# Hybrid decoder layer with 16 experts: the offset tables of the dynamic expert blocks made in the second block instead of the first

## The chip, the cores and the metric

One core of one Trainium2 chip runs the whole layer as one program. The metric is device time in microseconds, the median of several executions. Engines: PE (TensorE), DVE (VectorE), ACT (ScalarE), POOL (GpSimd, which here also issues nearly all transfers of the expert stage) and SP (SyncE).

## The reference, cut to what matters

The layer adds three mixers and an output projection to x and then a mixture of experts. Only the experts' stage is touched by the change:

```python
def hier_moe(h, wg, bg, we, be, w_gate, w_up, w_down):
    ...  # top-1 group of 4, then top-2 of its 4 experts: gates (T, 16), two nonzero per token
    for e in range(N_EXPERTS):
        hid = jax.nn.silu(t @ w_gate[e]) * (t @ w_up[e])
        y = y + gates[:, e:e + 1] * (hid @ w_down[e])
```

There are 1024 tokens of width 1024, 16 experts of width 256, float32 throughout.

## The kernel before, in words

The last quarter of the kernel is the expert stage. A token goes to two experts, so 2048 (token, expert) pairs are sorted on the chip into blocks of 128 pairs with one expert each. `moe` lists 23 blocks: four static ones (the first block of experts 0 to 3, known when the kernel is built) and 19 dynamic ones in `ORDER`, where P is an expert with two blocks and S an expert with one; which expert each of these is comes out of the routing. So 19 sets of expert weights are used (numbers 0 to 3 static, 4 to 18 dynamic), each of three 1 MB arrays: gate, up and down.

`moe_run` handles a block a in these steps. `gather(a)` (L1252, POOL) fetches the block's 128 tokens by an indirect transfer. `moe_xt` (L1263) transposes them on PE, and ACT and DVE split them in a high and a low half (L127, L128; the kernel multiplies float32 as three products of halves). `moe_gu` (L1277) is 24 matmuls with the gate and up weights, numbered n = 0 to 23; before number n it calls `mid(n)`. `moe_ht` and `moe_down` (L1289, L1305) transpose the result and multiply it with the down weights; ACT and DVE scale it into a page y (L1308, L1309); POOL adds the page into the output by an indirect transfer that accumulates (L1310, called a scatter below). While block a is multiplied, `splits(a+2)` splits the weights of a later expert into halves: ACT makes the high half (L127), DVE the low one by a subtraction (L128), and POOL makes one of the low halves of the down weights. `mw` holds four pairs of split buffers, so a split waits until PE has read the pair it replaces.

Raw weights land in a ring of ten 1 MB buffers (`raw_tile`, L1191). The first ten arrays are loaded by SP long before; all others are issued by POOL (L1212 for expert 3's up and down, L1217 for the dynamic ones), each waiting until the buffer that it overwrites has been split. `issue_after(K.last_gather)` keeps a group of loads behind the newest gather or scatter on POOL.

`route_map` makes the tables of the dynamic blocks in two parts. The first part (L1140 to L1180, before the first block) is a chain of small operations on DVE that ends in `sel`. The second part, after the `yield` (L1181), is `run(late)`: PE multiplies the slot table by `sel` and `selS` (L1120) and by two row vectors (L1185, L1186), DVE turns the results into offsets and gates (L1112 to L1130) and into `erow`, the experts' row numbers (L1188). Dynamic gathers need `og`; dynamic loads need a register loaded from `erow` (L1215); every scatter needs the offsets and gates, the static blocks' too.

The order on PE is the written order (`manual_schedule`, L1429). On ACT, DVE and POOL a planner sets the order at build time; each engine then works through its instructions in that order. In `moe_run` the second part of `route_map` and `loads(4)` stand in `mid` of block 0 at n = `MAP_AT` = 8 (L1362 to L1364); `loads(5)` stands at the end of block 0 and `loads(6)` at the end of block 1 (L1379, L1380).

Of the kernel before, what the change touches and what calls it, by code (L numbers as in the profile page):

```python
# [41 lines left out]
HT_AT = 12  # L42
ORDER = 'PSSPSSPSSPSSSSS'
YP = [0, 0, 0, 1]
MAP_AT = 8
DOWN_AT = 16
END_POOL = 6
END_PAGE = 3
# [214 lines left out]
def run(gen):  # L263
    for _ in gen:
        pass
# [832 lines left out]
def warm(K, n):  # L1098
    d = K.psum.tile([128, 1024], FT, name="warm", tag="sc")
    for m in range(n):  # L1100
        K.nc.tensor.matmul(d[:, :512].rearrange("p (a b) -> p a b", b=128), K.identb,
                           K.maskb.unsqueeze(1).to_broadcast([128, 4, 128]), start=True, stop=True)
# [146 lines left out]
def moe_gather(K, j):  # L1249
    nc = K.nc  # L1250
    xg = K.xpage.tile([128, D], FT, name="xg", tag="pg")
    K.last_gather = nc.gpsimd.indirect_dma_start(out=xg, out_offset=None, in_=K.td,  # L1252
                                 in_offset=bass.IndirectOffsetOnAxis(ap=K.slots[j][0], axis=0)).ins
    return xg


def moe_xt(K, xg, parts=1):
    nc = K.nc
    xT = [K.op.tile([128, KT, 128], FR, name="xT", tag="mx", bufs=4) for _ in range(2)]
    xv = xg.rearrange("p (d k) -> p k d", k=KT)  # L1260
    pt = K.psum.tile([128, KT, 128], FT, name="pt", tag="sc")
    for k in range(KT):
        nc.tensor.transpose(pt[:, k, :], xv[:, k, :], K.ident)  # L1263
    for z in range(parts):
        ks = slice(z * KT // parts, (z + 1) * KT // parts)
        split(K, xT[0][:, ks], xT[1][:, ks], pt[:, ks])
    return xT


def moe_gu(K, W, xT, mid):  # L1270
    nc, mp = K.nc, K.mp
    ps = K.psum.tile([128, 512], FT, name="pgu", tag="acc", bufs=2)
    order = [(k, t) for hf in range(2) for t in range(2) for k in range(hf * 4, hf * 4 + 4)] + [(k, 2) for k in range(KT)]
    for n, (k, t) in enumerate(order):
        mid(n)
        a, b = passes(xT, W[k // 4])[t]
        nc.tensor.matmul(ps, a[:, k, :], b[:, k % 4].rearrange("p a f -> p (a f)"), start=(n == 0), stop=(n == 23))  # L1277
    sg = mp.tile([128, 256], FT, name="sg", bufs=2)
    nc.scalar.activation(sg, ps[:, :256], AF.Silu)
    nc.vector.tensor_tensor(sg, sg, ps[:, 256:], op=OP.mult)  # L1280
    return sg


def moe_ht(K, hid):
    nc, mp = K.nc, K.mp
    hv = hid.rearrange("p (d k) -> p k d", k=2)
    pt = K.psum.tile([128, 4, 128], FT, name="pth", tag="tr")
    for k in range(2):
        nc.tensor.transpose(pt[:, k, :], hv[:, k, :], K.ident)  # L1289
    hT = [mp.tile([128, 2, 128], FR, name="hT", bufs=4) for _ in range(2)]  # L1290
    split(K, hT[0], hT[1], pt[:, :2, :])
    return hT


def moe_down(K, W, hT, j, spare=False):
    nc, mp = K.nc, K.mp
    yp = K.xpage if spare or YP[K.ny % len(YP)] else K.ypage
    K.ny += 1
    y = yp.tile([128, D], FT, name="y", tag="pg")
    wd = [z.rearrange("p a b c -> p (a b c)").rearrange("p (k d) -> p k d", k=2) for z in W[2]]  # L1300
    py = K.psum.tile([128, 1024], FT, name="py", tag="sc")
    for c in range(2):
        for t, (a, b) in enumerate(passes(hT, wd)):
            for k in range(2):
                nc.tensor.matmul(py[:, c * 512:(c + 1) * 512], a[:, k, :], b[:, k, c * 512:(c + 1) * 512],  # L1305
                                 start=(k == 0 and t == 0), stop=(k == 1 and t == 2))
    gt = K.slots[j][2]
    nc.scalar.activation(y[:, :512], py[:, :512], AF.Copy, scale=gt)  # L1308
    nc.vector.tensor_scalar(y[:, 512:], py[:, 512:], gt, None, op0=OP.mult)  # L1309
    K.last_gather = nc.gpsimd.indirect_dma_start(out=K.out, out_offset=bass.IndirectOffsetOnAxis(ap=K.slots[j][1], axis=0),  # L1310
                                 in_=y, in_offset=None, bounds_check=S + 127, compute_op=OP.add).ins


def moe_run(K, tiles, ex, main):
    n = len(tiles)
    first = {}
    for a, (l, j) in enumerate(tiles):
        first.setdefault(l, a)
    begins = {a: l for l, a in first.items()}
    xg, xT, hid = {}, {}, {}  # L1320

    def gather(a):
        if a < n:
            xg[a] = moe_gather(K, tiles[a][1])

    def loads(l):
        if l in first:
            if l >= len(ex):
                ex.append(Expert(K, None, tiles[first[l]][1] - NSTAT))
            with K.tc.issue_after(K.last_gather):  # L1330
                ex[l].loads()

    def splits(a):
        if a in begins:
            ex[begins[a]].splits(main and a >= n - END_POOL)

    def down(a):
        moe_down(K, ex[tiles[a][0]].W, hid[a], tiles[a][1], main and a >= n - END_PAGE)

    for a in range(3):  # L1340
        gather(a)
    if main:
        late = route_map(K)
        next(late)
        warm(K, WARM[2])
        xT[0] = moe_xt(K, xg[0], 2)
    with ExitStack() as st:
        for ins in [K.last_gather] + ([K.last_tab] if main else []):
            st.enter_context(K.tc.issue_after(ins))
        for l in range(3):  # L1350
            loads(l)
        splits(0)
        loads(3)
        splits(1)
        if not main:
            loads(4)
    if not main:
        xT[0] = moe_xt(K, xg[0], 2)
    for a in range(n + 1):
        if a < n:  # L1360
            def mid(m):
                if main and a == 0 and m == MAP_AT:  # L1362
                    run(late)
                    loads(4)  # L1364
                if m == HT_AT and a > 0:
                    hid[a - 1] = moe_ht(K, hid[a - 1])
                if m == XT_AT and a + 1 < n:
                    xT[a + 1] = moe_xt(K, xg[a + 1])
                if m == DOWN_AT and a == n - 1 and a > 0:
                    down(a - 1)  # L1370

            hid[a] = moe_gu(K, ex[tiles[a][0]].W, xT[a], mid)
            gather(a + 3)
            splits(a + 2)
        else:
            hid[n - 1] = moe_ht(K, hid[n - 1])
        if a > 0 and (a != n - 1 or DOWN_AT is None):
            down(a - 1)
        if a + 2 in begins:  # L1379
            loads(begins[a + 2] + 3)  # L1380


def moe(K, ex):
    tiles = [(l, l) for l in range(NSTAT)]
    p, q = 0, 2 * NPAIR
    for l, c in enumerate(ORDER, NSTAT):
        if c == "P":
            tiles += [(l, NSTAT + p), (l, NSTAT + p + 1)]
            p += 2
        else:  # L1390
            tiles.append((l, NSTAT + q))
            q += 1
    moe_run(K, tiles, ex, True)


def moe_rest(K, a=0):
    rv = K.nc.values_load(K.erow[0:1, NDYN + a:NDYN + a + 1], min_val=0, max_val=1)  # L1397
    with K.tc.If(rv > 0):
        moe_run(K, [(x - a, NSTAT + NALW + x) for x in range(a, NDYN - NALW if a else 1)], [], False)
        if not a:  # L1400
            moe_rest(K, 1)
# [204 lines left out]
```

## Time and profile before

| | |
|---|---|
| time, median of 3 runs | 940.19 us (939.62 to 940.92) |
| the profiled execution: its time | 938.4 us |
| the profiled execution: its span, first to last instruction | 936.7 us |
| mean granted TensorE clock | 0.941 |
| PE busy over the span | 827.5 us (88%) |
| DVE, ACT, POOL busy | 648.7, 494.5, 164.9 us |
| HBM read, written | 97.33 MB, 20.97 MB |

The expert stage lies between about 666 us and the end. The page's slices show shares of busy time in fortieths of the span (23.4 us each); in the timelines a row is a run of like instructions: start and length in us, engine, line, operation, tiles, shape and count, then in brackets how long the engine sat idle before and what released it. A q behind a queue or engine's name means its sequencer. One software queue (q0) carries all that POOL issues.

### The profile page before, as it was taken

How to read it: one execution, taken by the hardware profiler on the slowest of the kernel's cores; microseconds unless marked ns; L12 is line 12 of the kernel's file. 1: busy time of each engine (PE TensorE's matmuls, PEld its weight loads, DVE VectorE, ACT ScalarE, POOL GpSimd, SP SyncE). 2: the span in 40 equal slices, each digit the busy share in tenths (PEclk: the TensorE clock that was granted, in tenths of full speed). 3: DMA queues.
4: the chain of work that ended last, by engine and by line, in shares of the span. 5: the costliest groups of instructions: out<-in, count | busy, mean ns of one | idle time of the engine just before them, and what ended most of it. 6: DMA issues, size and time to landing. Idle time of an engine off the chain costs nothing. (4 is left out here: it accounts for less than half of the span.)

```text
span 936.7 us, 14405 instructions
## 1 busy us (share of the span) xinstructions
PE 827.5 (88%) x5300; PEld 721.2 (77%) x5300; DVE 648.7 (69%) x1442; ACT 494.5 (53%) x1095; POOL 164.9 (18%) x165
## 2 busy tenths in 40 slices
PE   5999999789778998899878899999889999999870
PEld 4999989688667987788767687888568888888760
DVE  6841556988997667767857666766768677787860
ACT  6743516114246665667757554232648677676740
POOL 5100000000000000000000000000446667664221
PEclk9999989669879999999988999999989999999995
DMA  8210100102002002001111218435389999998942
GB/s 266 72 45 2 47 1 25 39 1 57 12 0 69 1 1 68 1 1 40 61 30 49 91 68 330 187 129 209 119 319 327 331 362 309 371 311 293 333 70 47
DMA packets 46008, 119.30 MB, mean 127 GB/s; under 512 B 6670, under 2 KB 26220, under 8 KB 38636
## 3 DMA queue, kind: packets, MB, share of 16 engines
q0 software_dynamic: 13392, 73.41, 23.9%
q1 hardware_dynamic: 28588, 39.05, 12.8%
q10 hardware_dynamic: 3952, 5.86, 1.7%
q8 instruction: 44, 0.72, 0.3%
q14 instruction: 32, 0.26, 0.1%
HBM read 97.33 MB, written 20.97 MB: 126 GB/s over the span
## 5 line engine op out<-in xcount | busy, mean ns | idle before, releaser
L1277 PE MATMUL pgu<-mw,xT 128*128 128x512 f32 x552 | 140.9, 404 | 0.7 <-ACT xT L127 0.7
L128 DVE TENSOR_TENSOR mw<-mraw,mw 128x1024 fp32r<-128x1024 f32 x100 | 119.2, 1230 | 11.7 <-ACT mw L127 11.6
L1277 PEld LDWEIGHTS pgu<-mw,xT 128*128 128x128 f32 x552 | 102.8, 190 | 24.5 <-ACT xT L127 0.9
L127 ACT ACTIVATE mw<-mraw 128x1024 fp32r<-128x1024 f32 x114 | 113.7, 1051 | 15.0 <-PE pgu L1277 14.9
L249 PE MATMUL psA<-wh,hnh 128*128 128x384 f32 (+1 forms) x320 | 110.4, 345 | 1.0 <-ACT wh L127 0.9
L249 PE MATMUL psA<-wl,hnh 128*128 128x384 f32 (+1 forms) x320 | 109.9, 343 | 1.0 <-DVE wl L128 1.0
L249 PE MATMUL psA<-wh,hnl 128*128 128x384 f32 (+1 forms) x320 | 110.5, 345 | 0.2 <-DVE hnl L128 0.2
L879 PE MATMUL psO<-woh,mx 128*128 128x512 f32 (+1 forms) x272 | 87.1, 397 | 3.3 <-DVE mx L128 2.3
L584 DVE SCALAR_TENSOR_TENSOR mix<-mix,par 128x994 f32<-128x994 f32 (+29 forms) x60 | 75.9, 1265 | 2.1 <-ACT mix L581 1.3
L940 POOL IOTA iota<- 128x128 f32 x1 | 0.2, 238 | 434.9 <-DVE mix L612 434.9
L1305 PE MATMUL py<-mw,hT 128*128 128x512 f32 x276 | 67.4, 392 | 4.5 <-DVE y L1309 2.9
L1305 PEld LDWEIGHTS py<-mw,hT 128*128 128x128 f32 x276 | 51.7, 188 | 16.8 <-ACT hT L127 3.9
L249 PEld LDWEIGHTS psA<-wh,hnh 128*128 128x128 f32 x320 | 63.3, 198 | 1.6 <-ACT wh L127 1.3
L249 PEld LDWEIGHTS psA<-wl,hnh 128*128 128x128 f32 x320 | 63.3, 198 | 1.2 <-DVE wl L128 1.2
L249 PEld LDWEIGHTS psA<-wh,hnl 128*128 128x128 f32 x320 | 63.2, 197 | 0.6 <-DVE hnl L128 0.4
L716 DVE TENSOR_REDUCE nm<-sc 128x1 f32<-128x128 f32 (+7 forms) x64 | 46.9, 753 | 21.6 <-PE sc L712 17.8
L718 ACT ACTIVATE e<-sc,nm 128x128 f32<-128x128 f32 (+7 forms) x64 | 47.3, 740 | 25.5 <-DVE nm L716 21.7
L879 PEld LDWEIGHTS psO<-woh,mx 128*128 128x128 f32 x272 | 49.9, 192 | 12.7 <-DVE mx L128 2.8
L258 PE MATMUL psA<-hnh,wl 128*128 128x256 f32 x192 | 57.2, 298 | 0.0
L258 PE MATMUL psA<-hnl,wh 128*128 128x256 f32 x192 | 57.1, 297 | 0.0
L258 PE MATMUL psA<-hnh,wh 128*128 128x256 f32 x192 | 56.1, 292 | 0.2 <-DVE mix L554 0.2
L879 PE MATMUL psO<-wol,mx 128*128 128x512 f32 (+1 forms) x136 | 53.5, 394 | 0.0
(391 smaller groups left out, 1857.6 us busy)
## 6 DMA issues: line engine op xcount, KB each, us to landing
mraw<-in_expert_w_up_dram POOLq DMA_DIRECT2D x16, 1024.0 KB
mraw<-in_expert_w_down_dram POOLq DMA_DIRECT2D x16, 1024.0 KB
mraw<-in_expert_w_gate_dram POOLq DMA_DIRECT2D x15, 1024.0 KB
wraw<-in_w_in_dram SPq DMA_DIRECT2D x64, 128.0 KB
mix<-in_x_dram SPq DMA_DIRECT2D x8, 512.0 KB
wraw<-in_w_out_dram SPq DMA_DIRECT2D x16, 256.0 KB
h<-in_x_dram SPq DMA_DIRECT2D x8, 512.0 KB
out_dram<-h SPq DMA_DIRECT2D x8, 512.0 KB
```

The lines of the kernel that those rows point to most:

```text
L127: K.nc.scalar.activation(hi, src, AF.Copy)
L128: (eng or K.nc.vector).tensor_tensor(lo, src, hi.bitcast(FT), op=OP.subtract)
L249: nc.tensor.matmul(ps[:, :n], a[:, k, cs], b[:, k % 2, :n], start=(k == 0 and t == 0), stop=(k == KT - 1 and t == 2))
L258: nc.tensor.matmul(ps, a[:, k % 2, c0:c0 + 128], b[:, k, :], start=(k == 0 and t == 0), stop=(k == KT - 1 and t == 2))
L584: nc.vector.scalar_tensor_tensor(y[:, sh:], z[:, :S - sh], w(t), y[:, sh:], op0=OP.mult, op1=OP.add)
L716: nc.vector.tensor_reduce(nm, scs[m][:, :n], axis=AX.X, op=OP.max, negate=True)
L718: nc.scalar.activation(e[:, :n], scs[m][:, :n], AF.Exp, bias=nm, accum_out=sums[:, u, m:m + 1])
L879: nc.tensor.matmul(ps, a[:, k, :], b[:, k % 4, c0 % 512:c0 % 512 + c1 - c0], start=(k == 0 and t == 0), stop=(k == KT - 1 and t == 2))
L940: g.iota(t, allow_small_or_imprecise_dtypes=True, **kw)
L1277: nc.tensor.matmul(ps, a[:, k, :], b[:, k % 4].rearrange("p a f -> p (a f)"), start=(n == 0), stop=(n == 23))
L1305: nc.tensor.matmul(py[:, c * 512:(c + 1) * 512], a[:, k, :], b[:, k, c * 512:(c + 1) * 512], start=(k == 0 and t == 0), stop=(k == 1 and t ...
```

## The change

The second part of `route_map` moves from block 0 (before matmul 8 of its gate and up product) to block 1 (before matmul 2). `loads(4)` goes with it. `loads(5)` is traced right behind it instead of at the end of block 0. `loads(6)` stays at the end of block 1. The computation is the same.

```diff
-MAP_AT = 8
+MAP_AT = 2
...
     for a in range(n + 1):
         if a < n:
             def mid(m):
-                if main and a == 0 and m == MAP_AT:
+                if main and a == 1 and m == MAP_AT:
                     run(late)
                     loads(4)
+                    loads(5)
                 if m == HT_AT and a > 0:
                     hid[a - 1] = moe_ht(K, hid[a - 1])
...
-        if a + 2 in begins:
+        if a + 2 in begins and not (main and a == 0):
             loads(begins[a + 2] + 3)
```

## Rows read from the trace of the kernel before

**Rows 1.** The page's second part: busy tenths in 40 slices, PE and DMA.

```profile
PE   5999999789778998899878899999889999999870
DMA  8210100102002002001111218435389999998942
```

**Rows 2.** Stretches, PE from 679 us: engines' busy us (instructions), PEclk, DMA share, GB/s.

```profile
679.00:683.50 4.50, 0.18 (x1) 0.02 (x1) 4.09 (x14) 0.00 (x0) 2.19 (x2) 1.00 0.88 299
683.50:690.30 6.80, 6.79 (x27) 6.02 (x28) 1.37 (x10) 0.99 (x1) 3.31 (x4) 0.50 0.81 306
```

**Rows 3.** Timeline of PE, the first two blocks and one later half block.

```profile
677.05 2.14 PE L1277 MATMUL pgu<-mw,xT 128*128 128x512 f32 x8 [0.69 <-ACT xT L127]
683.51 1.02 PE L1120 MATMUL pio<-sel,tab 128*128 128x27 f32 x4 [4.33 <-DVE sel L1180]
...
685.49 2.08 PE L1277 MATMUL pgu<-mw,xT 128*128 128x512 f32 x4
687.36 1.91 PE L1263 MATMUL pt<-ident,xg 128*128 128x128 f32 x8
688.92 6.48 PE L1277 MATMUL pgu<-mw,xT 128*128 128x512 f32 x24
695.94 1.06 PE L1263 MATMUL pt<-ident,xg 128*128 128x128 f32 x8
696.75 3.05 PE L1277 MATMUL pgu<-mw,xT 128*128 128x512 f32 x12
...
702.40 2.98 PE L1277 MATMUL pgu<-mw,xT 128*128 128x512 f32 x12
705.22 0.39 PE L1289 MATMUL pth<-ident,sg 128*128 128x128 f32 x2
```

**Rows 4.** Timeline of POOL, the scatters at the end.

```profile
863.14 2.27 POOL L1310 DMA_INDIRECT out_dram<-y,os  x1 [8.97 <-DVE mw L128]
864.86 1.17 POOL L1217 DMA_DIRECT2D mraw<-in_expert_w_gate_dram  x1
...
882.41 1.65 POOL L1310 DMA_INDIRECT out_dram<-y,os  x1 [8.62 <-DMA out_dram<-y,os]
...
919.63 1.55 POOL L1310 DMA_INDIRECT out_dram<-y,os  x1 [5.41 <-issue]
```

**Rows 5.** Timeline of PE, its last matmuls.

```profile
908.09 3.02 PE L1305 MATMUL py<-mw,hT 128*128 128x512 f32 x12 [0.47 <-ACT hT L127]
```

**Rows 6.** Stretches, POOL alone: us, POOL busy (instructions), PEclk, DMA share, GB/s.

```profile
692.00:717.00 25.00, 14.90 (x13) 1.00 0.96 335
717.00:738.00 21.00, 12.68 (x10) 1.00 1.02 351
...
758.00:763.00 5.00, 3.84 (x5) 1.00 1.01 428
...
863.00:869.50 6.50, 4.01 (x4) 1.00 0.59 118
```

**Rows 7.** Timeline of DVE, the tables and the next subtractions.

```profile
683.13 0.24 DVE L1180 TENSOR_SCALAR sel<-iota,mz 128x27 f32<-128x27 f32 x1
...
684.77 0.17 DVE L1130 COPY ow<-pio 128x27 f32<-128x27 f32 x1
...
692.85 2.36 DVE L128 TENSOR_TENSOR mw<-mraw,mw 128x1024 fp32r<-128x1024 f32 x2 [1.26 <-ACT mw L127]
```

**Rows 8.** Timeline of POOL, dynamic gathers, loads and the first scatter.

```profile
685.04 1.02 POOL L1252 DMA_INDIRECT xg<-td,og  x1 [3.85 <-DVE ow L1130]
...
694.37 0.56 POOL L1217 DMA_DIRECT2D mraw<-in_expert_w_up_dram  x1 [3.85 <-DVE mw L128]
...
709.20 1.66 POOL L1310 DMA_INDIRECT out_dram<-y,ss  x1 [0.16 <-issue]
```

**Rows 9.** Timeline of POOL, a subtraction and the scatter behind it.

```profile
817.10 2.94 POOL L128 TENSOR_TENSOR mw<-mraw,mw 128x1024 fp32r<-128x1024 f32 x1 [1.12 <-ACT mw L127]
820.21 1.63 POOL L1310 DMA_INDIRECT out_dram<-y,os  x1 [0.17 <-issue]
```

## The prediction

> **What bounds the kernel now.** I read three views in this order: the slices of the page, the timeline of PE around the code that moves, and then, because PE is not the whole story, the timeline of POOL to the end.
>
> The slices show PE at eight or nine tenths through the expert stage and the transfer engines at nine in the same slices [rows 1]. Both could be the limit. The timeline of PE shows what the change aims at: after eight matmuls of block 0, PE stands still for 4.33 us until DVE has made `sel` [rows 3]. The stretches add a second cost of that gap: the granted clock was 1.00 while PE stood, and 0.50 (1.2 instead of 2.4 GHz) from 683.5 to 690.3 [rows 2]. Eight transposes took 1.91 us there and 1.06 later, four matmuls 2.08 us against 2.82 for twelve (702.40 to 705.22) [rows 3].
>
> But PE does not end the kernel. Its last matmuls end at 911.11 [rows 5]; the last scatter is issued 8.5 us later, at 919.63 [rows 4]. The scatters form a chain of their own: one waited 8.62 us on POOL for the transfer of the one before it [rows 4]. How long a scatter takes depends on the loads in front of it in the one queue that POOL fills, and that queue is full: share 1.02 from 717 to 738 [rows 6]. So the end is set by the queue and the chain of scatters. A gain on PE counts only as far as it lets the queue start its work earlier or fills holes in it.
>
> **What the change takes away on PE.** In place of 677.05 to 696.75 (the start of block 1's second half) I lay the same work at full speed [rows 3]: 24 matmuls of block 0 at 2.82 per twelve, 5.64; transposes of block 1, 0.81 (695.94 to 696.75); two matmuls of block 1, 0.47; the tables at their old price, 1.98 (683.51 to 685.49); ten matmuls, 2.35; two transposes, 0.39; eight more, 0.81. That is 12.45, so the second half of block 1 would start at 689.5 instead of 696.75: 7.2 us earlier. If the tables also run at the high clock, their half of the price is gone and it is 8.2. I expect no half clock, since nothing like a 4.33 us stop is left.
>
> Against this stands DVE. `sel` was ready at 683.37 [rows 7]; PE would ask for it at 677.05 + 0.1 + 5.64 + 0.81 + 0.47 = 684.1, so that wait is gone. But block 1's split of xT and the subtractions of expert 1's second half, 1.2 us each [rows 7], now fall into the same microseconds as DVE's part of the tables. In the order that the planner gives DVE, none, one or two of these can stand in front: 0 to 2.4 us, and PE waits for DVE within the tables. I take 1 us, near the lower half, since each is short and the operations of the tables come first in the code. PE gains 5 to 8 us, 6.7 as the middle value.
>
> **What it adds: the tables come later.** The first dynamic gather waited 3.85 us on POOL for `ow` and went at 685.04 [rows 8], 1.5 us after the tables began at 683.51 [rows 3]. Now they begin at 684.1, 0.6 later, or more with a DVE operation in front; at the high clock the two products before `ow` take less. So the gathers and the loads behind them on POOL start 0.2 to 3 us later; I take 0.9, 0.6 and a share of one subtraction. `loads(4)` and `loads(5)` are three transfers each, both groups behind the same gather; the register loads before them move along. What waits in front of them on POOL is only what waited there before. Nothing is short of weights for it: blocks 0 to 3 use loads that are already issued.
>
> **What the queue can use.** From 692 to 717 it moved 335 GB/s for 25 us, 8.4 MB [rows 6]. This is the stretch in which the later loads wait for subtractions that PE paces: the up load of expert 4 stood 3.85 us for one [rows 8]. With PE 6.7 us ahead these waits go, and the queue has always something to do. At the 351 GB/s of the full stretch behind it [rows 6] the 8.4 MB need 23.9 us: 1.1 us saved. But that stretch holds two scatters to six loads, the earlier one only one (the first is issued at 709.20 [rows 8]), and loads alone ran at 428 GB/s [rows 6], at which 8.4 MB need 19.6: 5.4 us saved. One scatter and a few gathers stand between; the estimate from both ends is 3.2 us. The queue's late start (0.9) is to be taken off that: 2.3.
>
> Further on one place is left where PE held the chain: the scatter at 820.21 was issued right behind a subtraction on POOL that had waited 1.12 us for ACT [rows 9]. ACT's splits follow PE's reads, so this wait ends earlier too; 0 to 1.1, I take 1.0. All else from 717 on is queue and chain, and moves along.
>
> The sum: 0.9 - 3.2 - 1.0 = -3.3 us. The profiled execution took 938.4 us and would take 935.1. It lies 1.8 us under the median of the runs; from 940.19 the same sum gives 936.9. PE's 6.7 us are more than twice that; the rest becomes lead of PE over the scatters and comes back as waits for pages at the end.
>
> **Rivals.**
>
> *PE is the bound after all.* If the chain follows PE because the queue has holes enough, the whole 5 to 8 us arrive: 940.2 - 6.7 = 933.5. For it speaks that PE is at nine tenths [rows 1], against it the 8.5 us at the end in which PE does nothing [rows 4, 5].
>
> *The queue gives nothing.* With the lower end (1.1 us), tables 2 us late and nothing at 820 the sum is +0.9; with 1.0 at 820 it is -0.1. That is 939 to 941, no change. For it speaks the share of 0.96 already between 692 and 717 [rows 6].
>
> The Trainium skill has a rule that speaks for this rival: DMA: Bandwidth & Descriptors, "Rules for kernel authors", says that an accumulating transfer next to another access of the same bytes must wait for the semaphore of the earlier one. By that rule the scatters can never overlap, whatever PE does, and the trace agrees (the 8.62 us wait for the scatter before [rows 4]).
>
> *Loads stand behind a waiting scatter (slower).* The change alters the order in which loads, gathers and scatters are traced, and with it the times by which the planner orders POOL. At 863.14 a scatter had kept POOL for 8.97 us and the loads of an expert stood behind it [rows 4]; the queue ran dry, share 0.59 for 6.5 us, 2.7 us lost [rows 6]. Each further place of this kind costs 2.7. One costs most of the gain (939.6); from the second on the kernel is slower: -3.3 + 5.4 = +2.1, 942.3. The same holds for the tables: if the first dynamic gather goes later than 685.04 + 3.2 + 1.0 = 689.2, the late start outweighs what the queue can use. For it speaks that POOL works strictly in its order; against it that only the first loads are moved, and by less than a block.
>
> That the change doesn't do what it says is not likely on PE, whose order is written by hand.
>
> **Chances.** The forecast (934.5 to 938.3) 0.53; the whole of PE's gain (932 to 934.5) 0.09; no change 0.21; slower 0.17. The smallest difference that the measurement of this kernel can tell is about 0.2%, 1.9 us. Faster by more than that is the forecast nearly whole and the first rival, 0.60; within it 0.22; slower 0.18. The range reaches from 932.5, below which half of the first rival lies, to 942.5, above which about half of the slower case lies. The forecast's own range is 934.5 to 938.3: tables 0.2 to 2 us late, 2 to 5 us out of the queue.
>
> **What the profile after would show.** On PE: 24 matmuls of block 0 and the transposes of block 1 without a gap, the tables at about 684 with a wait under 1 us, no stretch of clock 0.50 near 685, the second half of block 1 at 689 to 691. On POOL: the first dynamic gather at 685.3 to 688, the loads of expert 4 with no wait for a subtraction, the first scatter about 6 us earlier. From 692 on a share of 1.0 and more than 335 GB/s. At the end the last scatter near 916.3, and pages waited for longer than before on ACT or PE. I would be wrong if the first gather came after 689, if the low clock stayed, if the queue between 692 and 717 stayed at 335 GB/s, or if the queue had a new hole like the one at 863.

## The result, and the profile after

The changed kernel takes 947.03 us (median of 14 runs, 941.67 to 952.85), the kernel before in the same comparison 939.9 us (14 runs, 934.15 to 944.65). The ratio is 1.0081, with a 95% interval of 1.0054 to 1.0107: slower by 0.8%, where 936.9 us and a small gain had been forecast. The profiled execution took 946.58 us, its span is 945.0 us (before 936.7).

The page's second part for the changed kernel, busy tenths of PE and of the transfer engines; compare [rows 1]:

```profile
PE   5999999789678998999797999999899999999940
DMA  8210101102002002002203129362589898988942
```

PE is still at nine tenths in the expert stage; the transfer engines fall under nine in more slices than before. What the change aims at did happen. The timeline of PE (start, length, engine, line, operation, shape, count, and in brackets the idle time before with what ended it), to be laid beside [rows 3] and [rows 5]:

```profile
675.59 3.07 PE L1277 MATMUL pgu<-mw,xT 128*128 128x512 f32 x12 [0.69 <-ACT xT L127]
...
682.66 0.52 PE L1120 MATMUL pio<-sel,tab 128*128 128x27 f32 x4
...
684.17 0.21 PE L1185 MATMUL per<-sel,e 128*1 128x27 f32 x2 [0.56 <-DVE ow L1130]
...
687.83 3.05 PE L1277 MATMUL pgu<-mw,xT 128*128 128x512 f32 x12
...
906.62 3.01 PE L1305 MATMUL py<-mw,hT 128*128 128x512 f32 x12 [0.47 <-ACT hT L127]
```

And two stretches of PE around the tables (us, PE busy, granted clock, share of the transfer engines, GB/s), against [rows 2]:

```profile
683.00:686.00 3.00, 2.44 (x17) 1.00 0.16 68
686.00:690.00 4.00, 4.00 (x24) 1.00 0.57 166
```

The stop of 4.33 us is gone, the half clock too (1.00 instead of 0.50), and the second half of block 1 starts 12.24 us after block 0's first matmul (687.83 less 675.59) instead of 19.70. PE is 7.5 us ahead. At the end nothing of it is left: PE's last matmuls end at 909.63, 234.0 us after block 0's first one, just as before (911.11 less 677.05 is 234.1), and the last scatter goes only 18.3 us after that, where it went 8.5 us after it [rows 4, 5]. So the time has to be looked for on POOL and in its queue. POOL's timeline in the changed kernel, at the head of the dynamic blocks, in the middle and at the end:

```profile
684.21 2.07 POOL L1252 DMA_INDIRECT xg<-td,og  x1 [5.61 <-DVE tk L1124]
...
689.44 2.42 POOL L128 TENSOR_TENSOR mw<-mraw,mw 128x1024 fp32r<-128x1024 f32 x1
691.80 0.58 POOL L1217 DMA_DIRECT2D mraw<-in_expert_w_gate_dram  x1
...
700.11 2.46 POOL L1310 DMA_INDIRECT out_dram<-y,ss  x1 [0.17 <-issue]
...
716.63 1.80 POOL L1310 DMA_INDIRECT out_dram<-y,ss  x1 [6.02 <-DVE sg L1280]
...
811.38 1.94 POOL L1310 DMA_INDIRECT out_dram<-y,os  x1 [2.57 <-DMA out_dram<-y,os]
813.75 2.95 POOL L128 TENSOR_TENSOR mw<-mraw,mw 128x1024 fp32r<-128x1024 f32 x1 [0.44 <-ACT mw L127]
817.36 0.99 POOL L1252 DMA_INDIRECT xg<-td,og  x1 [0.66 <-PE pt L1263]
825.20 3.27 POOL L128 TENSOR_TENSOR mw<-mraw,mw 128x1024 fp32r<-128x1024 f32 x1 [6.85 <-ACT mw L127]
828.64 1.58 POOL L1310 DMA_INDIRECT out_dram<-y,os  x1 [0.17 <-issue]
829.70 1.16 POOL L1217 DMA_DIRECT2D mraw<-in_expert_w_gate_dram  x1
...
921.17 1.56 POOL L1310 DMA_INDIRECT out_dram<-y,os  x1 [5.27 <-DMA out_dram<-y,os]
927.95 1.56 POOL L1310 DMA_INDIRECT out_dram<-y,os  x1 [5.23 <-issue]
```

The first scatter goes at 700.11, 24.5 us after block 0's first matmul and 7.6 us earlier than before (709.20 less 677.05 is 32.2 [rows 8]). The second goes at 41.0 (716.63), where 41.7 had been the place before, so the lead lasts for one scatter (it takes 15.7 us to land, 7.9 before). From there the scatters fall behind. The worst place is the one at 828.64: it stands behind two subtractions of POOL and a gather, and the second subtraction waited 6.85 us for ACT's half of the split; the loads of the next expert (829.70) stand behind the scatter in turn. From the scatter before it, 17.3 us pass; the same step took 10.9 us before (809.29 to 820.21, [rows 9]).

Not all of that is the subtraction. A transfer has landed with the last update of its semaphore, which the trace has too; for the scatter at 811.38, issued behind three gathers, the view of the output's transfers says:

```profile
DMA to landing us min/median/max: 13.2/13.2/13.2
```

So it landed at 824.6, most of the 6.85 us passed while it was still under way, and the next scatter went 4.1 us after the landing. In the kernel before, these two parts are 9.1 and 1.9 us. POOL alone in a stretch, as in [rows 6]:

```profile
692.00:717.00 25.00, 13.62 (x14) 1.00 0.98 361
...
825.00:830.00 5.00, 4.63 (x3) 1.00 0.01 3
```

The queue is dry there (share 0.01). Two lines of the list of POOL's waits (what waited, for what: us in total, times, longest). The kernel before:

```profile
POOL out_dram L1310 <- DMA out_dram<-y,os: 23.4, 5, 8.6
...
POOL mw L128 <- ACT mw L127: 1.1, 1, 1.1
```

The changed kernel:

```profile
POOL out_dram L1310 <- DMA out_dram<-y,os: 45.2, 9, 9.3
POOL mw L128 <- ACT mw L127: 19.4, 7, 6.9
```

The second line is what is new: subtractions that wait for ACT, 19.4 us instead of 1.1. The first overstates the change, since the list puts some waits of a scatter for the one before it down to DVE or to nothing; all waits of scatters together are 81 us before and 86 after. Nothing in the diff touches the subtractions that wait, which lie 52 to 143 us behind the tables (the first that waits over 1 us goes at 734.43, the last at 825.20). What put them where they wait is the order on POOL.

### The profile page after: what moved, and what is told of

Read it like the earlier page. It is cut to its first block, busy times and chain, and to the rows that moved or that the text cites. A ratio compares the mean times of both kernels' runs of the same rounds, so it can differ in the third digit from the quotient of the medians.

```text
span 945.0 us, 14383 instructions
## 1 busy us (share of the span) xinstructions
PE 826.8 (87%) x5300; PEld 718.0 (76%) x5300; DVE 656.3 (69%) x1442; ACT 495.2 (52%) x1095; POOL 160.0 (17%) x165
## 5 line engine op out<-in xcount | busy, mean ns | idle before, releaser
L128 DVE TENSOR_TENSOR mw<-mraw,mw 128x1024 fp32r<-128x1024 f32 x100 | 128.3, 1323 | 11.6 <-ACT mw L127 10.7
L127 ACT ACTIVATE mw<-mraw 128x1024 fp32r<-128x1024 f32 x114 | 113.5, 1050 | 16.5 <-PE pgu L1277 11.3
L716 DVE TENSOR_REDUCE nm<-sc 128x1 f32<-128x128 f32 (+7 forms) x64 | 46.9, 752 | 19.5 <-PE sc L712 15.7
L879 PEld LDWEIGHTS psO<-woh,mx 128*128 128x128 f32 x272 | 50.4, 194 | 12.8 <-DVE mx L128 2.7
## 6 DMA issues: line engine op xcount, KB each, us to landing
mraw<-in_expert_w_gate_dram POOLq DMA_DIRECT2D x15, 1024.0 KB, 10.4
```

Of the source, the lines that this page charges most:

```text
L127: K.nc.scalar.activation(hi, src, AF.Copy)
L128: (eng or K.nc.vector).tensor_tensor(lo, src, hi.bitcast(FT), op=OP.subtract)
L716: nc.vector.tensor_reduce(nm, scs[m][:, :n], axis=AX.X, op=OP.max, negate=True)
L879: nc.tensor.matmul(ps, a[:, k, :], b[:, k % 4, c0 % 512:c0 % 512 + c1 - c0], start=(k == 0 and t == 0), stop=(k == KT - 1 and t == 2))
```

## What the planner did with the change

Read off the two traces, POOL's order from the second scatter on (S: scatter of a block, G: gather, g, u, d: loads of an expert's gate, up and down, M: POOL's subtraction for an expert; block and expert by number). Before:

```
S1 g7 u7 d7 M4 S2 G8 G9 G10 S3 g8 u8 d8 M5 G11 S4 g9 u9 d9 M6 S5 g10 u10 d10 M7
S6 G12 G13 G14 S7 g11 u11 d11 M8 G15 S8 g12 u12 d12 M9 S9 g13 u13 d13 M10
S10 G16 G17 G18 M11 S11 g14 u14 d14 G19 S12 ...
```

Changed:

```
S1 g7 u7 M4 d7 G8 G9 S2 G10 M5 G11 S3 g8 u8 d8 S4 g9 u9 d9 M6 M7 S5 g10 u10 d10 G12 G13 G14
S6 M8 G15 S7 g11 u11 d11 M9 S8 g12 u12 d12 M10 S9 g13 u13 d13 G16 G17 G18
S10 M11 G19 M12 S11 g14 u14 d14 S12 ...
```

Every gather from G8 on except G10 now stands ahead of one scatter behind which it stood, and subtractions go earlier: M5, M7 to M10 and M13 by one scatter, M12 by two. Ahead of the second scatter one place differs: gather 6 and M1 stand ahead of the first dynamic load (g4), which goes at 691.80, 16.2 us after block 0's first matmul, though the first dynamic gather goes at 8.6, only 0.6 us later than before (685.04 less 677.05 is 8.0).

**Theory.** The loss comes with this order alone; the places of the tables and of the loads would have paid as summed. **Rivals:** the tables themselves are too late; or PE's lead brings loads and scatters to collide in the queue.

## The experiments

In all kernels but e11 POOL's order in the expert stage is pinned: each of these instructions is ordered behind the one listed before it, for the planner only, with no wait added at run time. In e7, e9, e10 and e12 to e15 `issue_after` on the loads is taken off too, since the list says where they go. ACT and DVE stay with the planner, which fits their order to the list: in e2 ACT runs the same sequence of operations as in the changed kernel, and not that of the kernel before. So what a list costs includes what comes with it on these two engines. Pinning by itself moves nothing: in e8, whose list is the kernel's own, ACT, DVE and POOL keep their sequences in the expert stage. Line numbers are shifted by the helper (L1310 is L1339 there, L128 is L134, and so on).

```diff
+def pin(K, order):
+    prev = None
+    for key in order.split():
+        if key[0] in "GSM":
+            ins = K.noted[key[0]][int(key[1:])]
+        else:
+            ins = K.noted["L"][3 * int(key[1:]) + "gud".index(key[0]) - 10]
+        if prev is not None:
+            K.tc.add_manual_dep(ins, prev.name, mybir.DependencyInfo(mybir.DependencyClass.NoSync,
+                                                                     mybir.DependencyReason.DATA), reason="pin")
+        prev = ins
...
+        pin(K, POOL_ORDER)
         order.close()
```

The table has all kernels. Each ratio is to the kernel before as it ran in the same comparison (medians 939.9 to 942.18). The last column is worked out: the span less the start of block 0's first matmul, in the profiled execution, one of each kernel. It helps because that matmul starts anywhere from 674.77 to 685.42 us, though no diff touches what lies ahead of it, and this spread is in the single times.

| kernel | median, us | ratio to before (95%) | block 0 to the end, us |
|---|---|---|---|
| before | 939.9 | | 259.7 |
| changed | 947.03 | 1.0081 (1.0054 to 1.0107) | 269.4 |
| e1: changed, POOL's order of before | 937.55 | 0.9963 (0.9941 to 0.9985) | 259.6 |
| e2: before, POOL's order of changed | 955.16 | 1.0155 (1.013 to 1.018) | 274.5 |
| e3: changed, order of before up to S1 | 949.4 | 1.0094 (1.0065 to 1.0122) | 271.5 |
| e4: changed, order of before from S1 on | 936.36 | 0.995 (0.993 to 0.997) | 257.5 |
| e5: changed, eight of its gathers put back | 948.21 | 1.0087 (1.0049 to 1.0125) | 271.8 |
| e6: changed, only its subtractions put back | 947.25 | 1.0092 (1.006 to 1.0124) | 268.8 |
| e7: e4, four experts' loads ahead of a scatter | 948.68 | 1.0099 (1.0066 to 1.0133) | 268.8 |
| e8: before, a stop on PE in block 1 | 943.65 | 1.0032 (1.0008 to 1.0057) | 264.5 |
| e9: changed, even order from S1 on | 934.06 | 0.9926 (0.9902 to 0.995) | 254.5 |
| e10: before, even order from S1 on | 927.54 | 0.9851 (0.9808 to 0.9893) | 250.0 |
| e11: before, tables at the end of block 0 | 945.42 | 1.0049 (1.002 to 1.0079) | 264.8 |
| e12: changed, even order, head of before | 933.62 | 0.992 (0.9889 to 0.9952) | 256.1 |
| e13: before, even order, head of changed | 937.82 | 0.9958 (0.9939 to 0.9977) | 255.0 |
| e14: e9 again | 934.5 | 0.991 (0.988 to 0.9941) | 257.9 |
| e15: e10 again | 932.38 | 0.989 (0.9859 to 0.9922) | 250.9 |

Several came out beside what had been expected of them: e2 (955.16 us, not 945 to 949), e3 (949.4, not 943 to 948), e4 (936.36, better than 938), e7 (948.68, at most 942), e8 and e9 between their two ranges, e10 (faster than e9, not slower), e13 (937.82, at most 936) and e15 (932.38, at most 930).

**The change without its order, the order without the change (e1, e2).** One edit each: the list that is pinned.

```diff
+POOL_ORDER = 'G0 G1 G2 G3 u3 M0 d3 G4 G5 g4 G6 u4 d4 M1 G7 ...'   # e1: before's list in the changed kernel
+POOL_ORDER = 'G0 G1 G2 G3 u3 M0 d3 G4 G5 G6 M1 g4 u4 d4 G7 ...'   # e2: the changed kernel's list in before
```

> The changed kernel, with the order of GpSimd's gathers, loads, subtractions and scatters in the expert stage pinned to that of the kernel before. Theory O (the order of GpSimd costs the time): the loss is gone, and what the prediction summed is left, 3 us faster than before, 935 to 939 us beside 940. Theory L (the late tables or TensorE's lead cost the time, whatever GpSimd's order): as the changed kernel, 945 to 949 us.

> The kernel before, tables in block 0 as ever, with GpSimd's order pinned to that of the changed kernel. Theory O: 945 to 949 us, as slow as the changed kernel although nothing of the tables has moved. Theory L: as before, 939 to 941 us.

With the order of before the changed kernel is faster than before by 0.15 to 0.59%, 1.4 to 5.6 us. With the order of the changed kernel the kernel before loses 1.55%, with its tables where they always were. The list of POOL's waits in e1 and then in e2:

```profile
POOL mw L134 <- ACT mw L133: 1.1, 1, 1.1
```

```profile
POOL mw L134 <- ACT mw L133: 25.5, 8, 6.9
```

The waits follow the order and not the tables. That speaks for the theory against both rivals: e1 has the late tables and PE's lead, and loses nothing. (e2 loses more than the changed kernel: its second scatter goes 46.0 us after block 0's first matmul, 4.3 later than before, since in it M1 stands ahead of the first dynamic load without PE's lead.) PE's last matmuls in e1:

```profile
902.65 3.02 PE L1334 MATMUL py<-mw,hT 128*128 128x512 f32 x12 [0.47 <-ACT hT L133]
```

They end 229.3 us after block 0's first (905.67 less 676.40), 4.8 us sooner than before, and the kernel still ends 259.6 us after it, as before.

**Which part of the order (e3, e4).** The two lists are exchanged at the second scatter, S1.

```diff
-... G5 G6 M1 g4 u4 d4 G7 ... S1 g7 u7 M4 d7 G8 G9 S2 ...
+... G5 g4 G6 u4 d4 M1 G7 ... S1 g7 u7 M4 d7 G8 G9 S2 ...   # e3
+... G5 G6 M1 g4 u4 d4 G7 ... S1 g7 u7 d7 M4 S2 G8 G9 ...   # e4
```

> The changed kernel, GpSimd's order pinned to that of before up to the second scatter, and to that of the changed kernel behind it. In the trace of the changed kernel the chain of scatters is level with before at the second scatter and about 10 us late at the twelfth. Theory O with the loss in the later order: 943 to 948 us, 2.5 us better than the change at most. Theory O with the loss in the first loads: 936 to 940. Theory L: 945 to 949.

> The changed kernel, GpSimd's order pinned to that of the changed kernel up to the second scatter, and to that of before behind it. Theory O with the loss in the later order: 938 to 941 us. Theory O with the loss in the first loads (six microseconds later at expert 4): 944 to 948. Theory L: 945 to 949.

The head, with its late first load, costs nothing here (e4 is level with e1); all of the loss lies behind S1, in an order of instructions that the diff doesn't touch. The traces say the same: from the second scatter to the last, the list of before takes 200.9 us in the kernel before, 201.4 in e1 and 200.1 in e4; the list of the changed kernel takes 211.3 in the changed kernel, 211.2 in e2 and 214.3 in e3. The step at which the changed kernel lost most, in POOL's timeline of e4:

```profile
805.22 2.53 POOL L1339 DMA_INDIRECT out_dram<-y,os  x1 [3.21 <-DVE mw L134]
...
812.42 2.77 POOL L134 TENSOR_TENSOR mw<-mraw,mw 128x1024 fp32r<-128x1024 f32 x1
815.36 1.63 POOL L1339 DMA_INDIRECT out_dram<-y,os  x1 [0.17 <-issue]
```

It takes 10.1 us instead of 17.3: the three gathers stand behind the first of the two scatters again, and M12 behind the second.

**Gathers or subtractions (e5, e6).** e5 puts back the eight gathers that had gone ahead of S2, S6 and S10 (G11, G15 and G19 to G22 stay ahead) and leaves the subtractions; e6 puts back the subtractions and leaves all gathers.

```diff
-d7 G8 G9 S2 G10 ... G12 G13 G14 S6 ... G16 G17 G18 S10 M11
+d7 S2 G8 G9 G10 ... S6 G12 G13 G14 ... S10 G16 G17 G18 M11   # e5
-G10 M5 G11 S3 g8 u8 d8 S4 g9 u9 d9 M6 M7 S5 ... S10 M11 G19 M12 S11
+G10 G11 S3 g8 u8 d8 M5 S4 g9 u9 d9 M6 S5 ... S10 G19 M11 S11   # e6, and M8 to M10, M12, M13 too
```

> The changed kernel with its own GpSimd order, but the gathers that it had moved ahead of scatters 2, 6 and 10 put back behind these scatters (8 gathers). Theory G (a gather moved ahead leaves the queue without work while the next scatter waits): most of the loss goes, 939 to 943 us beside 941 for before. Theory M (the subtractions that wait for ScalarE in front of scatters and loads cost it): 945 to 949, as the changed kernel.

> The changed kernel with its own GpSimd order, but the subtractions of experts 5 to 13 put back behind the loads that they followed before, so that no scatter or load waits behind one that waits for ScalarE. Theory M: 939 to 944 us (the longest such stop was 6.85 us ahead of scatter 11, which went 4.1 us after the landing before it instead of 0.8). Theory G: 945 to 949.

Neither brings anything back, but for different reasons. In e5 the subtraction M12 still holds the scatter (POOL's timeline):

```profile
827.34 3.35 POOL L134 TENSOR_TENSOR mw<-mraw,mw 128x1024 fp32r<-128x1024 f32 x1 [6.99 <-PE pth L1318]
830.85 1.62 POOL L1339 DMA_INDIRECT out_dram<-y,os  x1 [0.16 <-issue]
```

The scatter before it had landed after 9.9 us, at 820.9; the next one went 10.0 us after that. In e6 POOL waits for ACT's splits not once, but three gathers stand ahead of the first of these two scatters, and a fourth, which waits until PE has transposed the block whose buffer it overwrites, ahead of the second:

```profile
770.24 1.62 POOL L1339 DMA_INDIRECT out_dram<-y,os  x1 [0.32 <-issue]
778.47 0.99 POOL L1280 DMA_INDIRECT xg<-td,og  x1 [6.61 <-PE pt L1292]
783.82 1.59 POOL L1339 DMA_INDIRECT out_dram<-y,os  x1 [4.36 <-DVE mw L134]
```

13.6 us lie between these scatters; the same two (S6 and S7) stood 10.2 us apart before. The gather's wait of 6.61 us costs nothing: the first scatter took 12.8 us to land (9.4 before, and 9.0 in e5, where the three gathers stand behind it), until 783.0, and the second went 0.8 us after that. What costs are the three gathers whose transfers are ahead of the scatter in the queue. The landings of all scatters in the traces, from the second to the last, in us:

| kernel | whole | scatters in transfer, issue to landing | from a landing to the next issue |
|---|---|---|---|
| before | 200.9 | 181.5 | 19.4 |
| changed | 211.3 | 188.4 | 23.0 |
| e5 | 213.8 | 179.6 | 34.2 |
| e6 | 209.5 | 191.6 | 17.9 |

So either kind is enough, each in its own way. With the gathers ahead (e6) the scatters land later; with the subtractions ahead (e5) POOL comes late to the next scatter. In the changed kernel both happen, about two thirds of the loss in the transfers. They don't add up, since a subtraction can wait while a longer transfer is still under way.

**Loads ahead of the scatter, to keep the queue full (e7).** If a dry queue is the loss, loads might be put in front:

```diff
-S2 G8 G9 G10 S3 g8 u8 d8 M5
+S2 G8 G9 G10 g8 u8 d8 S3 M5      # and for experts 11, 14, 17 ahead of S7, S11, S15
```

> As e4, but at the four places where two scatters follow each other with no loads between, the next expert's loads stand ahead of the second scatter. If the queue's empty stretches bound the kernel, the about 5 us that it stands empty there in e4 are filled: 930 to 934 us beside 936 for e4 and 941 for before. If the chain of scatters bounds it by each scatter's own latency, the loads ahead of a scatter make it later: 936 to 942.

12 us slower than e4 by the medians. POOL's timeline, at the first place that was changed:

```profile
740.74 0.58 POOL L1241 DMA_DIRECT2D mraw<-in_expert_w_down_dram  x1
741.87 1.66 POOL L1339 DMA_INDIRECT out_dram<-y,ss  x1 [0.55 <-DMA out_dram<-y,ss]
...
757.20 1.97 POOL L1339 DMA_INDIRECT out_dram<-y,os  x1 [9.24 <-DVE mw L134]
```

15.3 us for this step of the chain, where e4 has 8.1 (735.98 to 744.07). The three loads, the last at 740.74, are in the queue ahead of the scatter at 741.87, and only a gather follows it: the scatter lands behind the loads, 14.5 us after its issue, the next one waits for it, and at the end the queue runs dry (share 0.01 from 757 to 759). The step behind it is shorter in turn (7.4 us against 11.3), so that the two together cost 3.3 us more than in e4. Work in the queue ahead of a scatter delays the chain; behind it, it is hidden by the chain's own wait.

**How far PE counts (e8).** In the kernel before, its order pinned, 20 matmuls on scratch data stop the real work in block 1 for about as long as `sel` does in block 0.

```diff
+                if main and a == 1 and m == 4:
+                    warm(K, 20)
```

> The kernel before with its own GpSimd order pinned and 20 idle matmuls (4.3 us at 0.215 each) more on TensorE in block 1, behind the tables. If TensorE's time at this place sets the end: 4 us slower, 945 us beside 941. If the queue and the scatters set it: 0 to 1.5 us slower, 941 to 942.5.

PE's timeline shows the stop:

```profile
699.15 4.49 PE L1107 MATMUL warm<-maskb,identb 128*128 128x512 bf16 x20
```

The loss is 0.32%, 3.0 us (0.8 to 5.4 by the interval), and 4.8 us from block 0 to the end in the profile, where the first scatter is already 3.0 us later than before. So a delay of 4.49 us on PE is paid, at least in part. Whether it weighs more than a lead isn't shown: some 7 us of lead gain 1.4 to 5.6 (e1).

**Another place, the same fate (e11).** The tables at the end of block 0, which removes the stop as well; nothing is pinned.

```diff
-MAP_AT = 8
+MAP_AT = 23
```

> The kernel before with one number changed, the tables before matmul 23 of block 0 instead of 8, loads traced as before, no order pinned. The planner gives GpSimd an order with gathers ahead of scatters and subtractions in front of scatters again, as in the changed kernel (not the same one). If such an order is what costs: 944 to 949 us, although the stop on TensorE is gone. If the place of the loads of expert 5 or the second block is what costs: 936 to 940.

Slower too, by 0.5%. The planner's order again has subtractions and gathers ahead of scatters, which fits, though nothing is pinned here to show that they are the cause; the list of POOL's waits:

```profile
POOL mw L128 <- ACT mw L127: 17.6, 6, 4.9
```

**An even order by hand (e9, e10, and again e14, e15).** From S1 to S16 every scatter but S2 (one load) gets two or three loads and about one gather behind it, and no subtraction is brought forward. e9 and e14 are the changed kernel, e10 and e15 the kernel before.

```diff
+S1 g7 u7 d7 M4 S2 G8 G9 g8 S3 u8 d8 G10 M5 S4 g9 u9 G11 M6 S5 d9 g10 G12 M7 S6 u10 d10 G13
+S7 g11 u11 G14 M8 S8 d11 g12 G15 M9 S9 u12 d12 G16 M10 S10 g13 u13 d13 S11 G17 g14 u14 M11 S12 ...
```

> The changed kernel with GpSimd's order from scatter 1 on written by hand: two or three loads and about one gather behind every scatter up to scatter 16, instead of three loads behind some and none behind others. If the time of the chain is the sum over scatters of the longer of two things, the work that stands in the queue in front of a scatter and the about 7 us that a scatter takes from issue to the next one's issue on an empty queue, then an even spread is best: 5 to 11 us less than e4 (936), 925 to 931. If only the order of gathers against scatters counts, as e4: 935 to 938.

> The same even order on the kernel before (tables in block 0, with the stop on TensorE). If the change itself, at a fixed order, is worth its 3 us (e1), this is 2 to 5 us slower than e9. If the place of the tables is worth nothing, it is level with e9.

Both beat both kernels, and the kernel before gains more. Two stretches of POOL, from the first scatter to the eleventh and from there to the last, in the kernel before:

```profile
709.20:809.30 100.10, 66.03 (x51) 1.00 0.99 337
809.30:919.60 110.30, 47.12 (x37) 0.98 0.81 253
```

and in e10:

```profile
709.60:804.60 95.00, 66.41 (x49) 1.00 1.01 344
804.60:912.80 108.20, 50.12 (x40) 1.00 0.86 273
```

The 210.4 us from the first scatter to the last become 203.2, at a higher share in both halves. The scatters land sooner: from the second to the last they are 169.4 us in transfer instead of 181.5. That e10 beats e9, though PE is not ahead there, was a miss: it had been expected to be the slower one.

**What the change costs at the even order (e12 to e15).** The square of both kernels with both heads (the list up to S1), on one chip.

```diff
-... G5 G6 M1 g4 u4 d4 G7 ... S1 (even)
+... G5 g4 G6 u4 d4 M1 G7 ... S1 (even)   # e12: in the changed kernel; e13: the reverse in before
```

> The changed kernel with POOL's head as in the kernel before (up to the scatter of block 1) and the even order by hand behind it: POOL's order is then, instruction for instruction, that of the kernel before at the even order (927.54 us in its runs), and only the place of the tables is that of the change. Theory 'the head of POOL's order makes the 6.5 us': 925 to 930, level with it, or 2 to 4 us faster, by the lead of PE. Theory 'the place of the tables itself makes them (the order of ACT and DVE that comes with it)': 932 to 936, level with the changed kernel at the even order (934.06).

> The kernel before with POOL's head as in the changed kernel and the even order behind it: the other corner of the same square. Theory 'head': 932 to 936. Theory 'place of the tables': 925 to 930.

> The changed kernel at the even order once more, on the chip of the other three. If the 6.5 us between this and the kernel before at the even order lay between two chips or chance, both come out level here; else 932 to 936.

> The kernel before at the even order once more, on the chip of the other three: 925 to 930, 1.2 to 1.6 per cent under the kernel before, if the earlier result is one of the kernel and not of the chip.

Neither theory holds alone. By the medians three corners are level (932.38, 933.62, 934.5, intervals overlapping) and only e13 lies above them (its interval still touches those of e12 and e14), so of the 6.5 us between e9 and e10 some 2 are left, within the noise. By the table's last column the kernel before with its own head stands alone: 250.0 and 250.9, against 254.5 to 257.9 for the other four runs. The traces show where. In e13 the head puts M1 ahead of g4 with nothing of PE's lead to pay for it (POOL's timeline):

```profile
696.61 2.96 POOL L134 TENSOR_TENSOR mw<-mraw,mw 128x1024 fp32r<-128x1024 f32 x1 [4.53 <-ACT mw L133]
699.52 0.57 POOL L1241 DMA_DIRECT2D mraw<-in_expert_w_gate_dram  x1
```

In e14, e9 and e12 it is near the end, and not on POOL's list. One place lies with ACT and DVE. The timelines of ACT, DVE and POOL in e14, at the page of block 18:

```profile
888.48 1.25 ACT L1337 ACTIVATE y<-py,ow 128x512 f32<-128x512 f32 x2
890.37 1.40 DVE L1338 TENSOR_SCALAR y<-py,ow 128x512 f32<-128x512 f32 x2
891.40 1.60 POOL L1339 DMA_INDIRECT out_dram<-y,os  x1 [11.51 <-DVE y L1338]
```

and in e15:

```profile
884.23 0.68 ACT L1337 ACTIVATE y<-py,ow 128x512 f32<-128x512 f32 x1
885.51 0.74 DVE L1338 TENSOR_SCALAR y<-py,ow 128x512 f32<-128x512 f32 x1
890.92 1.79 POOL L1339 DMA_INDIRECT out_dram<-y,os  x1 [8.79 <-DVE mw L134]
```

In e15 ACT and DVE scale page 18 between two groups of splits; in e14 the planner puts it, with the next page's, behind the second group, and the scatter waits 11.51 us, the last 2 of them for the page (it goes 2.8 us after the landing, 0.8 in e15). From the scatter before it, 13.4 us pass in e14 (878.02 to 891.40) and 10.9 in e15 (879.99 to 890.92). So moving the tables changes the planner's order on ACT and DVE too. The larger place is the scatter of block 19, in e14 and then in e15:

```profile
898.14 3.67 POOL L1339 DMA_INDIRECT out_dram<-y,os  x1 [5.14 <-DVE sg L1309]
```

```profile
897.99 1.57 POOL L1339 DMA_INDIRECT out_dram<-y,os  x1 [5.28 <-DVE mw L134]
```

It takes POOL longer and lands after 9.7 us instead of 6.2, so that the next step is 10.4 us in e9, 10.5 in e12 and 10.4 in e14, against 6.9 in e10 and 7.0 in e15. Why is not shown. What all this is worth in the median stays open: 2 us on one chip, 6.5 in another comparison, and no run pins ACT and DVE.

## Why the prediction was wrong

**Right, on PE.** The stop and the half clock are gone; 12.45 us had been summed for the stretch without a wait, and 12.24 were measured with one of 0.56 us within the tables for `ow`, where 1 us had been taken. PE's gain is 7.5, within the 5 to 8.

**Right, on the tables.** The first dynamic gather is 0.6 us later, of 0.2 to 3. The queue between 692 and 717 moved 361 GB/s at a share of 0.98, instead of 335. The bound of 689.2, from which on the late start would decide, was not touched (684.21).

**The sum.** It gave -3.3 us with POOL's order as it was; e1, which is that case, measured -1.4 to -5.6 us by its interval. The trace bears out one term and not the path to the end. The queue moved 384 GB/s between 692 and 717, at which 8.4 MB need 21.8 us: the 3.2 us saved that had been taken. But the first scatter, issued 5.4 us earlier, took 13.3 us to land instead of 7.9, so that at the second one e1 is only 0.8 us ahead (40.8 us after block 0's first matmul, 41.7 before). The term of 1.0 at the scatter of 820.21 gave nothing: the subtraction waits 1.1 us in e1 as before, and the step is 11.2 us instead of 10.9. At the nineteenth scatter e1 is 1.9 us ahead, at the last 0.4, and from block 0 to the end it takes 259.6 us beside 259.7. So the agreement is of the medians alone, and in part luck. "A gain on PE counts only as far as it lets the queue start its work earlier or fills holes in it" is borne out by e1 (PE done 4.8 us sooner, the end where it was); of a loss on PE it says nothing, and e8 shows that one is paid.

**Wrong: the step "All else from 717 on is queue and chain, and moves along", and with it "only the first loads are moved, and by less than a block".** It did not move along: from the second scatter to the last, 200.9 us became 211.3. The second sentence kept the chance of the slower rival at 0.17. That rival had the cause (the times by which the planner orders POOL, which works strictly in order) and a neighbour of the mechanism (loads behind a scatter that waits). What it had not was the reach: the loads of two experts were traced later, and the planner rearranged gathers and subtractions up to the gather at 851.73, on ACT and DVE too. e3 and e4 show that the whole loss lies there. Its price was mis-sized in the same way. 2.7 us for each new place was read at a load behind a scatter [rows 4, 6]; the new places are gathers and subtractions ahead of a scatter, and the worst cost 6.3 (17.26 less 10.92). The last of the prediction's own signs of being wrong came true there: a new hole in the queue (825 to 830). The rival's two places gave 2.1 us over the time before; 7.1 were measured (947.03 less 939.9), 9.7 from block 0 to the end.

**What was there to be read.** The trace before has one such place: the subtraction at 817.10 that waited 1.12 us for ACT with a scatter behind it [rows 9]. It was counted as a gain to come (1.0). It is the very place (the step from the eleventh scatter to the twelfth) at which the changed kernel lost most. The order that decides was planned when the kernel was built, so the cost of a new one could only be guessed at from the trace; e2 gives one sample of it, 1.55% for a plausible order, with nothing else in the source changed.

The rule of the Trainium skill in DMA: Bandwidth & Descriptors, "Rules for kernel authors" (an accumulating transfer waits for the semaphore of the earlier one on the same bytes), held in every run. The traces agree: no scatter is issued less than 0.27 us after the landing of the one before. It had been weighed for the rival of no change alone; it bears on the slower one as much, since steps that can't overlap add up, and a step that has grown is not made good behind it.

## What to carry to other kernels

Where a planner orders an engine, an edit to one place is an edit to all that is planned behind it: compare the orders of both kernels on each planned engine before believing any sum, or pin the order and measure the edit alone. In a chain of transfers that can't overlap, ask two things of whatever stands ahead of a scatter: does its own transfer go ahead in the queue (a gather, a group of loads), and can the issuing engine still be busy with it when the scatter before has landed (a subtraction that waits)? If the order can be written by hand, try that first: here it gave 1.1 to 1.5% (e10, e15), more than the edit gave at the old order (0.15 to 0.59%, e1).

## What the runs showed of the hardware

Scatters with nothing else in the queue follow each other at 6.8 us (914.33, 921.17 and 927.95 in the changed kernel), nearly all of it transfer: 6.0 to 6.1 us pass from issue to landing, and POOL waits 5.2 to 5.3 us at each. With the loads that have to come along the step is longer: 9.5 us on the mean of the first sixteen in e10 (709.61 to 862.00), 15.3 at the place shown of e7.

What stands ahead of a scatter in the queue shows in its landing: 6.0 us with nothing, 13.2 behind three loads and three gathers (811.38 in the changed kernel), 14.5 at the place shown of e7.

4.49 us of stop on PE cost 0.8 to 5.4 us in e8; some 7 us of lead gained 1.4 to 5.6 in e1 and had gone by the end in the changed kernel.

Executions of the same code reach the expert stage at times up to 10.7 us apart (674.77 to 685.42), so a single profile is better read from a mark in the code than from its start.
